# Three moves at the head of a hybrid encoder block: the second norm's spread, the third norm's sums, and a copy of the stream

## The chip, the cores and the metric

The kernel runs on one core of a Trainium2 chip. A core has five engines that run beside each other, each through its own list of instructions in order: TensorE (PE in the profile, with PEld for its weight loads), VectorE (DVE), ScalarE (ACT), GpSimd (POOL) and SyncE (SP, which here only issues transfers). They wait for each other through semaphores. The metric is the device time of one execution in microseconds. Three runs of the kernel before took 1533.51, 1535.86 and 1537.61 us, a median of 1535.86.

## The reference

The block takes 1024 frames of 1024 features, puts 16 learned meta tokens ahead of them, and runs one layer of two parts, each on a normalised stream and each added back to it.

```python
def rmsnorm(x, g):
    xf = x.astype(jnp.float32)
    y = xf * lax.rsqrt(jnp.mean(xf * xf, axis=-1, keepdims=True) + EPS)
    return (y * g.astype(jnp.float32)).astype(x.dtype)
...
    proj = up @ w_in
    (ml_q, ml_k, ml_v, ml_o, ml_i, ml_f, rt_q, rt_k, rt_v, rt_g) = jnp.split(proj, offs, axis=-1)
...
    rq = rotary(rt_q.astype(jnp.float32).reshape(b, lp, RT_HEADS, RT_DQK), pos)
    rk = rotary(rt_k.astype(jnp.float32).reshape(b, lp, RT_HEADS, RT_DQK), pos)
...
    h = jnp.concatenate([meta, x], axis=1)
    for l in range(DEPTH):
        h = h + token_mixer(rmsnorm(h, norm_mix_g[l]), ...)
        h = h + channel_mixer(rmsnorm(h, norm_ffn_g[l]), w_up[l], w_gate[l], ffn_conv_w[l], w_down[l])
    return rmsnorm(h, norm_final_g)[:, N_META:]
```

The token mixer projects the normalised stream to queries, keys, values and gates for eight heads: four of an mLSTM (with a convolution on queries and keys and exponential gates) and four of a retention (with rotary positions on queries and keys). The channel mixer is a gated MLP with a convolution. Only the first norm and the first products of the token mixer matter here.

## The kernel before

**Number form.** The products run in a fast 32-bit format that keeps fewer bits than float32. So each operand is split in a high part (a cast on ACT, names with `h` or `hi`) and a low part (original minus high part, on DVE, names with `l` or `lo`), and a product is done as high x high, high x low and low x high. Larger products are saved by a Winograd-style scheme with seven products instead of eight; it needs sums of quarters of the normalised stream, named S1 to S4.

**The head.** The stream lies in four tiles `x11`, `x12`, `x21`, `x22` (token half, then feature half), features on the partitions. It arrives and is normalised in five ranges of tokens (`RNG`: 144, 128 and 256 tokens of the first half, 272 and 256 of the second). For each range there are three steps:

- `norm_sums`: the squares are added (L855 on ACT, L859 or L863, L867 and L870 on DVE), PE adds them over the partitions (L826, tiles `pca0` to `pca4`), ACT takes the root (L828) and DVE the reciprocal (L829).
- `norm_rows`: PE hands the reciprocals to all partitions, the "spread" (L838, tiles `pra0` to `pra4`).
- `norm_split`: DVE scales the stream by it (L890, eight instructions), ACT casts the high parts (L891), DVE makes the low parts (L895).

In the rows below the tile's last digits are left out, so `pra`, `pca` and `pv` stand for all ranges. Between these steps PE does the first products on what is ready: `v4_group(c)` makes the values and gate columns of head 4 for chunk c (tile `pv4_c`, L952, 24 products of 264 columns), with the weights `w0hi` and `w0lo`; `v4_group(0)` does it for the 16 meta tokens in plain float32 with 32-column tiles (L938, eight products on `ug` and `w0raw`, named the meta products). Their four partial sums are added into `vz` by `quads`: a copy on ACT (L924) and three adds on DVE (L927). `q4_pair` makes queries and keys of head 4 for the first 272 tokens (tiles `pq4000` and `pq4100`, L977, 48 products in three passes over high and low parts); it calls `norm_sums` and `norm_rows` of the third range between its passes. `q4_group` makes them for the other tokens (L901 to L903).

**Behind the head.** `usum` forms S1 to S4 on DVE in the tiles of the stream, and `usplit` splits them (L1822 on ACT, L1823 on DVE). S1 is first formed in `s1`, two tiles that take the slots A1 and A2. S4's sums end up in `x12`, and a copy of them (L1844) goes to two other tiles, named `s4`, from which S4 is split. When S1 has been split, the slots A1 and A2 are reused for the rotary position tables `rot`, loaded by `tables_load(4)` (L1134 and L1135). The products of the output gate of head 4 (`po4x`, `po4y`, L911 to L913) then run in seven steps n = 0 to 6 over the blocks 11, 12, S2, S1, S3, S4 and 22; their results are collected in `sig`: a copy on ACT for n = 0 (L1000), a negated copy on ACT for n = 2 and 3 (L1002), an add on DVE for the others (L1004). Beside them run the rotary products of head 4 (L1209 to L1214) and `gates`, a chain of small DVE and ACT instructions on the gate columns. From there on PE goes through the query, value and output-gate weights of the other heads, the scans over the chunks, the output projection and the MLP.

**What sets the order.** Weights come in through slots (`raw...`, L328 on SP's queue); a load is issued when its slot's last reader is done, and SP issues in order, so a load that waits holds up those behind it. A helper `after(a, b)` sets instruction a behind b on its engine without a semaphore; the last instruction of a kind is kept in `last`. Where nothing is said, a list scheduler with its own cost model orders each engine's instructions when the program is built. From the output gate of head 4 on (`dealt`, `pinned`) the order is that of a planner which deals side work between PE's steps.

Of the kernel before, what the change touches and what calls it, by code (L numbers as in the profile page):

```python
# [20 lines left out]
META = 16  # L21
# [68 lines left out]
def body(ctx, tc, h_in, vecs, cst, mask_in, rot, w_v0, w_vp, w_g, w_out, w_up, w_gate, w_down, out):  # L90
# [14 lines left out]
    def after(later, first):  # L105
        dep(later, first, False)

    last = {}
# [118 lines left out]
    w0raw = (A1, A2)  # L227
# [651 lines left out]
    def norm_rows(r):  # L879
        norms[r] += (rms_rows(norms[r][1], None, "upd"),)  # L880
# [40 lines left out]

    def quads(dst, pv, n):
        yield
        AC.copy(dst, pv[:META, :n])  # L924
        yield
        for j in range(1, 4):
            V.tensor_tensor(dst, pv[32 * j:32 * j + META, :n], dst, ALU.add)  # L927
# [3 lines left out]
    def v4_group(c, tag, between=None):  # L931
        t0, L = CH[c]
        nv = 264
        pv = pp(f"pv4_{c}", tag)
        if c == 0:
            for i in range(2):
                for j in range(4):
                    PE.matmul(pv[32 * j:32 * j + 32, :nv], ug[:, 4 * i + j, :], w0raw[i][:, j * nv:(j + 1) * nv],  # L938
                                     start=i == 0, stop=i == 1, tile_position=(0, 32 * j))
            t = vz[:META, 264:264 + nv]  # L940
            spawn(quads(t, pv, nv))
            V.tensor_copy(gts[:META, :, 0, :], t[:, DV:].rearrange("p (a b) -> p a b", a=2))
            return
        half = c > 4
        j0 = t0 - 512 * half
        for i, j in ((0, 0), (0, 1), (1, 0)):
            if i and between:
                between()
            for kb in range(KB):
                u = UB[f"{half + 1}{kb // 4 + 1}"][i]  # L950
                o = kb % 4 * nv
                m = PE.matmul(pv[:, :nv], u[:, kb % 4, j0:j0 + L], (w0hi, w0lo)[j][kb // 4][:, o:o + nv], start=i + j + kb == 0, stop=i == 1 and kb == KB - 1, skip_group_check=True)  # L952
                if i and between:
                    after(m, last["rows"])
        AC.copy(vtile[4][half][:, (c - 1) % 4 * VW:(c - 1) % 4 * VW + DV], pv[:, :DV])
        V.tensor_copy(gts[:, :, c, :], pv[:, DV:nv].rearrange("p (a b) -> p a b", a=2))
# [9 lines left out]
    def q4_pair(half, j0, j1, tags, between):  # L966
        w = [need(("q4", i), 1 - i) for i in range(2)]
        pt = [pp(f"pq4{i}{half}{j0}", tags[i])[:, :j1 - j0] for i in range(2)]
        for p, (a, b) in enumerate(((0, 0), (0, 1), (1, 0))):
            if p == 2:  # L970
                between()
            for i in range(2):
                if p == 2 and i:
                    norm_rows(2)
                for kb in range(KB):
                    u = UB[f"{half + 1}{kb // 4 + 1}"][b]
                    m = PE.matmul(pt[i], w[i][kb // 4][a][:, kb % 4 * P:(kb % 4 + 1) * P], u[:, kb % 4, j0:j1], start=p + kb == 0, stop=p == 2 and kb == KB - 1, skip_group_check=True)  # L977
                    if p == 2:
                        after(m, last["rows" if i else "sums"])
        AC.copy(raws[0][:, half * 512 + j0:half * 512 + j1], pt[0])  # L980
        yield
        after(AC.copy(raws[1][:, half * 512 + j0:half * 512 + j1], pt[1]), last["cast"])
# [825 lines left out]
    def part(x, i):  # L1808
        return s1[i] if x == "S1" else xf[x][:, 2 * i:2 * i + 2]
# [31 lines left out]
    x12 = [vslot(2 + i, f"s4_{i}").rearrange("p (k j) -> p k j", k=2) for i in range(2)]  # L1841
    tables_load(4)
    for i in range(2):
        G.tensor_copy(x12[i], part("12", i))  # L1844
    s1[:] = x12
    need(("o", 4, 1))
    usplit("S4", "S1", "uh2", "ul2")
# [719 lines left out]
```

## Time and profile before

| | |
|---|---|
| median of three runs | 1535.86 us (1533.51 to 1537.61) |
| profiled execution | 1534.49 us, span 1532.7 us |
| granted PE clock, mean | 0.994 |
| PE busy | 1491.9 us, 97% of the span |
| DVE, ACT, POOL busy | 71%, 49%, 6% |
| mean DMA rate | 146 GB/s |

The profile is that of one execution. A row of the timeline has the start in us from the span's start, the busy time in us, the engine, the line, the operation, out<-in by the program's names, sizes, and the number of instructions merged in it; in brackets stands the idle time of the engine before it and what ended it. Matmuls overlap, so a row of several lasts less than the sum of its parts. A float32 product counts as two instructions in these rows.

### The profile page before, as it was taken

The numbers are of one execution on the slowest core, as the hardware profiler recorded it, in microseconds if no ns is written. First come the engines' busy times: TensorE is split into PE (matmuls) and PEld (weight loads), VectorE is DVE, ScalarE is ACT, GpSimd is POOL, SyncE is SP. The second block draws the span as 40 slices with busy tenths as digits, with TensorE's granted clock in tenths as the row PEclk, the third lists the DMA queues.
The fourth block names the chain that finished last, engine by engine and source line by source line (L and its number), as shares of the span: only waits on it lengthen the run. The fifth ranks groups of instructions, "written<-read, shape, count | busy, mean of one in ns | idle before, by whom it ended". The sixth has DMA issues, their size and how long they took to land.

```text
span 1532.7 us, 25492 instructions
## 1 busy us (share of the span) xinstructions
PE 1491.9 (97%) x9929; PEld 1351.0 (88%) x9929; DVE 1089.5 (71%) x2087; ACT 754.8 (49%) x1453; POOL 84.7 (6%) x159
## 2 busy tenths in 40 slices
PE   6979999999999999999999999999999999999997
PEld 5978999999999999997888988999999999888887
DVE  5875777767777768756868697677666666778657
ACT  4455655564655445544454465444444444434443
POOL 1020000000000000000000001222220000000000
PEclk9999999999999999999999999999999999999999
DMA  6022245323542354598333237787872224933313
GB/s 231 1 83 57 84 138 182 126 93 116 174 138 84 124 179 166 192 373 301 111 110 133 82 118 212 206 213 196 200 183 84 79 80 146 382 100 114 97 42 111
DMA packets 104586, 223.81 MB, mean 146 GB/s; under 512 B 10520, under 2 KB 33760, under 8 KB 104288
## 3 DMA queue, kind: packets, MB, share of 16 engines
q1 hardware_dynamic: 89824, 191.68, 37.3%
q0 software_dynamic: 8448, 23.07, 7.4%
q10 hardware_dynamic: 6192, 7.41, 1.4%
q8 instruction: 78, 1.28, 0.3%
q14 instruction: 44, 0.36, 0.1%
HBM read 178.05 MB, written 67.15 MB: 160 GB/s over the span
## 4 chain that ended last, share of the span: by engine, by line
PE 88%; DVE 6%; DMA 3%; ACT 2%; issue 1%; SPq 0%; DVEq 0%; ACTq 0%
PE pdx L913 3%; PE pdx L912 3%; PE pdx L911 3%; PE pup_x L912 2%; PE pup_x L913 2%; PE pup_x L911 2%; PE pga_x L911 2%; PE pga_x L912 2%; PE pga_x L913 2%; PE pdy L913 2%; PE pdy L912 2%; PE pdy L911 2%; PE n L1602 2%; PE pwx L913 2%; PE u L1600 2%; PE pwx L911 2%
## 5 line engine op out<-in xcount | busy, mean ns | idle before, releaser
L782 ACT CAST hi_up<-raw_up 128x512 fp32r<-128x512 f32 (+1 forms) x52 | 36.4, 719 | 107.3 <-PE pga_z L912 61.1
L911 PE MATMUL pup_x<-uh_g,hi_up 128*128 128x256 f32 (+1 forms) x240 | 67.6, 284 | 1.2 <-ACT uh_g L1964 1.2
L783 DVE TENSOR_TENSOR lo_up<-raw_up,hi_up 128x512 fp32r<-128x512 f32 (+1 forms) x52 | 41.2, 808 | 38.1 <-ACT hi_up L782 37.3
L783 DVE TENSOR_TENSOR lo_ga<-fraw_ga,hi_ga 128x512 fp32r<-128x512 f32 (+1 forms) x52 | 41.8, 807 | 36.7 <-ACT hi_ga L782 36.5
L912 PE MATMUL pup_x<-ul_g,hi_up 128*128 128x256 f32 (+1 forms) x240 | 67.7, 284 | 0.1
L913 PE MATMUL pup_x<-uh_g,lo_up 128*128 128x256 f32 (+1 forms) x240 | 66.7, 283 | 0.0
L783 DVE TENSOR_TENSOR lo_d<-rd,hi_d 128x1024 fp32r<-128x1024 f32 (+1 forms) x34 | 37.6, 1112 | 32.8 <-ACT hi_d L782 32.7
L782 ACT CAST hi_ga<-fraw_ga 128x512 fp32r<-128x512 f32 (+1 forms) x52 | 36.4, 719 | 45.5 <-PE pup_z L912 24.3
L913 PE MATMUL pdx<-uh_d,lo_d 128*128 128x512 f32 (+1 forms) x156 | 57.9, 375 | 0.0
L912 PE MATMUL pdx<-ul_d,hi_d 128*128 128x512 f32 (+1 forms) x156 | 57.8, 374 | 0.0
L782 ACT CAST hi_d<-rd 128x1024 fp32r<-128x1024 f32 (+1 forms) x34 | 32.3, 959 | 49.3 <-PE pdy L912 32.5
L913 PE MATMUL pdy<-uh_d,lo_d 128*128 128x512 f32 x132 | 51.9, 393 | 0.0
L912 PE MATMUL pdy<-ul_d,hi_d 128*128 128x512 f32 x132 | 51.7, 392 | 0.0
L911 PE MATMUL pdx<-uh_d,hi_d 128*128 128x512 f32 (+1 forms) x156 | 48.5, 372 | 0.0
L911 PE MATMUL pdy<-uh_d,hi_d 128*128 128x512 f32 x132 | 47.9, 389 | 0.0
L911 PEld LDWEIGHTS pup_x<-uh_g,hi_up 128*128 128x128 f32 x240 | 45.7, 191 | 2.3 <-ACT uh_g L1964 1.4
L911 PE MATMUL pga_x<-uh_g,hi_ga 128*128 128x512 f32 x120 | 47.5, 396 | 0.0
L912 PE MATMUL pga_x<-ul_g,hi_ga 128*128 128x512 f32 x120 | 47.5, 396 | 0.0
L913 PE MATMUL pga_x<-uh_g,lo_ga 128*128 128x512 f32 x120 | 47.1, 393 | 0.0
L912 PEld LDWEIGHTS pup_x<-ul_g,hi_up 128*128 128x128 f32 x240 | 45.8, 191 | 1.0 <-DVE ul_g L1965 0.3
L913 PEld LDWEIGHTS pup_x<-uh_g,lo_up 128*128 128x128 f32 x240 | 45.1, 190 | 0.8
L662 POOL DMA_DIRECT2D wsd<-w_down_d x33 | 19.9, 748 | 383.4 <-DVE s2up L2192 382.7
(1698 smaller groups left out, 5758.1 us busy)
## 6 DMA issues: line engine op xcount, KB each, us to landing
raw_up<-w_up_d SPq DMA_DIRECT2D x22, 512.0 KB, 5.2
fraw_ga<-w_gate_d SPq DMA_DIRECT2D x22, 512.0 KB, 4.2
acts<-cv SPq DMA_DIRECT2D x44, 256.0 KB, 4.3
wsd<-w_down_d POOLq DMA_DIRECT2D x44, 256.0 KB, 6.6
rd<-wsd SPq DMA_DIRECT2D x22, 512.0 KB, 3.5
raw_w<-w_out_d SPq DMA_DIRECT2D x20, 512.0 KB, 6.9
wsw<-raw_w SPq DMA_DIRECT2D x32, 256.0 KB, 3.6
raw_m<-w_out_d SPq DMA_DIRECT2D x14, 512.0 KB, 4.0
```

Of the source, the lines that this page charges most:

```text
L662: dep(G.dma_start(x, y), last["pace"], True)
L782: AC.copy(hi[:, o:o + n], x)
L783: V.tensor_tensor(lo[:, o:o + n], x, hi[:, o:o + n].bitcast(F32), ALU.subtract)
L911: m.append(PE.matmul(pt, ah, xh_, start=first and k == 0, stop=False, skip_group_check=True))
L912: PE.matmul(pt, ah, xl_, start=False, stop=False, skip_group_check=True)
L913: m.append(PE.matmul(pt, al, xh_, start=False, stop=last and k == n - 1, skip_group_check=True))
L1600: PE.matmul(up[:, :nv], kw[:L], v, start=True, stop=True)
L1602: PE.matmul(pn[:L, :nv], pt[:L, :L], v, start=True, stop=c == 0)
```

## The change

It has three parts. In `v4_group` the meta products are set behind the second norm's spread, and in `quads` the copy of their result behind the last cast of a norm. In `q4_pair` the third norm's sums come ahead of the first pass of the query and key products, not ahead of the third, and its spread behind the first pass, not in the middle of the third; the passes are set behind them. And the copy of S4's sums into their own tiles is done by ACT and no longer by POOL.

```diff
     def quads(dst, pv, n):
         yield
-        AC.copy(dst, pv[:META, :n])
+        m = AC.copy(dst, pv[:META, :n])
+        if not dealt[0]:
+            after(m, last["cast"])
         yield
...
             for i in range(2):
                 for j in range(4):
-                    PE.matmul(pv[32 * j:32 * j + 32, :nv], ug[:, 4 * i + j, :], w0raw[i][:, j * nv:(j + 1) * nv],
-                                     start=i == 0, stop=i == 1, tile_position=(0, 32 * j))
+                    after(PE.matmul(pv[32 * j:32 * j + 32, :nv], ug[:, 4 * i + j, :], w0raw[i][:, j * nv:(j + 1) * nv],
+                                    start=i == 0, stop=i == 1, tile_position=(0, 32 * j)), last["rows"])
...
         for p, (a, b) in enumerate(((0, 0), (0, 1), (1, 0))):
-            if p == 2:
+            if p == 0:
                 between()
+            if p == 1:
+                norm_rows(2)
             for i in range(2):
-                if p == 2 and i:
-                    norm_rows(2)
                 for kb in range(KB):
                     u = UB[f"{half + 1}{kb // 4 + 1}"][b]
                     m = PE.matmul(pt[i], w[i][kb // 4][a][:, kb % 4 * P:(kb % 4 + 1) * P], u[:, kb % 4, j0:j1], start=p + kb == 0, stop=p == 2 and kb == KB - 1, skip_group_check=True)
-                    if p == 2:
-                        after(m, last["rows" if i else "sums"])
+                    after(m, last["rows" if p else "sums"])
...
     for i in range(2):
-        G.tensor_copy(x12[i], part("12", i))
+        AC.copy(x12[i], part("12", i))
     s1[:] = x12
```

The number of products stays the same; ACT has two instructions more and POOL two fewer. Beyond 125 us only six products of one group at the start of the MLP change places among themselves. In the head and just behind it the scheduler comes to another order at several places. Three of them follow; a row is a line, an operation, out<-in with the program's buffer numbers, and a size, and x4 stands for four like it in a row.

PE at the end of the products of chunk 1 (`pv_1`), before: the meta products (`pv_0`) are dealt among the last low-weight products, and the spread of the second norm (`pra_285`) comes behind them.

```order
L952 MATMUL pv_1_254<-w0lo_109,u12h 128x264
L938 MATMUL pv_0_309<-w0raw_104,ug 32x264
L952 MATMUL pv_1_254<-w0lo_109,u12h 128x264
L938 MATMUL pv_0_309<-w0raw_104,ug 32x264 x2
L952 MATMUL pv_1_254<-w0lo_109,u12h 128x264
L938 MATMUL pv_0_309<-w0raw_104,ug 32x264
L938 MATMUL pv_0_309<-w0raw_105,ug 32x264
L952 MATMUL pv_1_254<-w0lo_109,u12h 128x264
L938 MATMUL pv_0_309<-w0raw_105,ug 32x264 x2
L838 MATMUL pra_285<-cs,rcola_273 128x128
```

The same place now:

```order
L954 MATMUL pv_1_254<-w0lo_109,u12h 128x264 x4
L838 MATMUL pra_285<-cs,rcola_273 128x128
L954 MATMUL pv_1_254<-w0hiq,u11l 128x264 x4
L954 MATMUL pv_1_254<-w0hik,u12l 128x264 x4
L940 MATMUL pv_0_309<-w0raw_104,ug 32x264 x4
L940 MATMUL pv_0_309<-w0raw_105,ug 32x264 x4
```

The spread has moved ahead of all meta products, and these stand together behind the products of chunk 1.

PE at the fourth norm's spread (`pra_514`), which no edit names, before: it stands near the end of the query products for tokens 272 to 528 (`pq_542`), and 26 products follow it (three of `pq_542`, 23 of the keys, `pq_568`) until the first product of the second half (`pv_5`).

```order
L901 MATMUL pq_542<-u12h,hi_q_0_0_354 128x256
L902 MATMUL pq_542<-u12l,hi_q_0_0_354 128x256
L903 MATMUL pq_542<-u12h,lo_q_0_0_355 128x256
L838 MATMUL pra_514<-cs,rcola_450 128x16
L838 MATMUL pra_514<-cs,rcola_450 128x128 x2
L901 MATMUL pq_542<-u12h,hi_q_0_0_354 128x256
L902 MATMUL pq_542<-u12l,hi_q_0_0_354 128x256
L903 MATMUL pq_542<-u12h,lo_q_0_0_355 128x256
L902 MATMUL pq_568<-u11l,hi_q_1_0_362 128x256
```

Now:

```order
L901 MATMUL pq_568<-u11h,hi_q_1_0_362 128x256
L902 MATMUL pq_568<-u11l,hi_q_1_0_362 128x256
L903 MATMUL pq_568<-u11h,lo_q_1_0_363 128x256
L838 MATMUL pra_514<-cs,rcola_450 128x16
L838 MATMUL pra_514<-cs,rcola_450 128x128 x2
L901 MATMUL pq_568<-u12h,hi_q_1_0_362 128x256
L902 MATMUL pq_568<-u12l,hi_q_1_0_362 128x256
L903 MATMUL pq_568<-u12h,lo_q_1_0_363 128x256
```

It has moved into the middle of the key products: 12 products follow it until `pv_5`.

ACT behind the sums S1 to S4 (`s_0` of L1822 is the first half of S1 or of S4 by the name on the left; `raw_o4a` and `raw_o4b` are weights of the output gate), before:

```order
L1822 CAST uS3h<-x_120 128x1056 x2
L474 CAST hi_o_4_0_873<-raw_o4b 128x512 x2
L964 COPY rawk<-pq_823 128x256
L1000 COPY sig<-po4x_887 128x258
L1822 CAST uS1h<-s_0_609 128x1056
L1822 CAST uS1h<-s_1_610 128x1056
L1000 COPY sig<-po4x_901 128x256
L1822 CAST uS4h<-s_0_855 128x1056
L1822 CAST uS4h<-s_1_856 128x1056
L474 CAST hi_o_2_0_863<-raw_o4a 128x512
```

and now, with the two copies (L1845) in between:

```order
L1823 CAST uS3h<-x_120 128x1056 x2
L1845 COPY s_0_855<-x_121 128x1056
L474 CAST hi_o_4_0_873<-raw_o4b 128x512 x2
L966 COPY rawk<-pq_823 128x256
L1001 COPY sig<-po4x_887 128x258
L1845 COPY s_1_856<-x_121 128x1056
L1823 CAST uS1h<-s_0_609 128x1056
L1823 CAST uS1h<-s_1_610 128x1056
L1823 CAST uS4h<-s_0_855 128x1056
L1823 CAST uS4h<-s_1_856 128x1056
L474 CAST hi_o_2_0_863<-raw_o4a 128x512
L1001 COPY sig<-po4x_901 128x256
```

The copies stand ahead of the casts of `hi_o_4` and of S1, and one copy out of `po4x` has gone behind a weight cast.

SP's queue at the same place, before (`A_4` are the two position tables):

```order
L328 DMA raw_vp_21_1268<-w_vp_d 128x1024
L328 DMA raw_vp_22_1270<-w_vp_d 128x1024
L1134 DMA A_4_857<-rot_d 128x1040
L1135 DMA A_4_858<-rot_d 128x1040
L328 DMA raw_q0b<-w_g_d 128x512 x2
```

and now:

```order
L1135 DMA A_4_857<-rot_d 128x1040
L1136 DMA A_4_858<-rot_d 128x1040
L328 DMA raw_vp_21_1268<-w_vp_d 128x1024
L328 DMA raw_vp_22_1270<-w_vp_d 128x1024
L328 DMA raw_q0b<-w_g_d 128x512 x2
```

The tables have moved ahead of the two value weights.

## The prediction

> **What bounds the kernel now.** I read the page first, then busy time by stage, then the chain of work that ended last, and last the timeline of the first 110 us, where the moved instructions stand. The page:
>
> ```profile
> span 1532.7 us, 25492 instructions
> ...
> PE 1491.9 (97%) x9929; PEld 1351.0 (88%) x9929; DVE 1089.5 (71%) x2087; ACT 754.8 (49%) x1453; POOL 84.7 (6%) x159
> ...
> PE 88%; DVE 6%; DMA 3%; ACT 2%; issue 1%; SPq 0%; DVEq 0%; ACTq 0%
> ```
>
> TensorE (PE) carries the kernel. The change adds and removes no product, so it can only fill PE's idle time, and that lies in few places. Busy time by stage (stretch, length, then PE, PEld, DVE, ACT, POOL, granted clock, DMA share, GB/s):
>
> ```profile
> 0.00:40.00 40.00, 28.23 (x172) 24.28 (x173) 23.74 (x53) 18.48 (x30) 7.36 (x20) 1.00 0.64 221
> ...
> 77.00:102.00 25.00, 17.93 (x133) 16.07 (x132) 17.45 (x27) 13.98 (x26) 9.43 (x2) 0.91 0.37 127
> ...
> 125.00:1532.00 1407.00, 1386.68 (x9148) 1252.46 (x9146) 999.11 (x1906) 695.23 (x1349) 64.61 (x134) 1.00 0.48 150
> ```
>
> PE idles 11.8 us before 40 and 7.1 us between 77 and 102; in the 1407 us after 125 it loses 20 us in all. So what is won or lost by 102 should reach the end. The chain of work names what holds the second stretch, and prices a product (36 in 4.51 us, 0.125 us each):
>
> ```profile
> 39.08 4.51 PE pv L952 x36
> ...
> 84.90 10.07 DMA A<-rot_d
> ```
>
> **The second norm's spread.** Seven of the eight meta products stand between the last pv4_1 products with the lower weights and the spread (pra1, which hands the scales to all partitions). DVE waits for it:
>
> ```profile
> 18.06 0.42 PE L952 MATMUL pv<-w0lo,u12h 128*128 128x264 f32 x1
> ...
> 21.99 0.49 PE L838 MATMUL pra<-cs,rcola 128*128 128x128 f32 x2
> ...
> 22.52 2.15 DVE L890 SCALAR_TENSOR_TENSOR x<-x,vec,pra 128x128 f32<-128x128 f32 x8 [4.81 <-PE pra L838]
> ...
> 24.99 0.76 PE L952 MATMUL pv<-w0hiq,u11h 128*128 128x264 f32 x4 [0.98 <-ACT u11h L891]
> ```
>
> Now four products are left ahead of pra1: 18.06 + 4 x 0.125 = 18.56, and DVE scales 0.53 later (22.52 - 21.99), at 19.1, done at 21.25. PE does eight more products (to 19.8) and then the meta products in one piece. Their price is between two rows: 3.65 us if each costs what it does now (21.99 - 18.06 less three products, for seven, times 8/7) and 1.07 us if they run like sixteen such passes that do stand together:
>
> ```profile
> 82.83 1.07 PE L722 MATMUL pvm<-raw_vm,ug 128*32 128x256 f32 x16
> ```
>
> The second has the same form, so I take it with 0.4 us for the change of shape: PE is free at 21.3. ACT's cast u11h, after the first half of the scaling (20.2) and a copy, ends by 21.0. The pv4_2 products start at 21.3, not 24.99. The copy of vz, moved behind the casts, has DVE adds as its only reader, and those have moved later too.
>
> **The third norm.** Now the sums (pca2) stand ahead of all 48 query products, and the spread (pra2) behind the first 16:
>
> ```profile
> 26.78 1.21 DVE L867 TENSOR_TENSOR sqr<-sqr,sqr 128x1024 f32<-128x1024 f32 x1
> 28.39 0.67 DVE L870 TENSOR_TENSOR sqr<-sqr 128x512 f32<-128x512 f32 x1
> 28.98 2.48 DVE L479 TENSOR_TENSOR lo_q<-raw_q,hi_q 128x512 fp32r<-128x512 f32 x4
> ...
> 32.04 0.95 PE L826 MATMUL pca<-cs,sqr 128*128 128x1 f32 x8
> ...
> 34.58 3.22 DVE L890 SCALAR_TENSOR_TENSOR x<-x,vec,pra 128x256 f32<-128x256 f32 x8 [1.09 <-PE pra L838]
> ...
> 35.19 1.12 ACT L474 CAST hi_o<-raw_o4a 128x512 fp32r<-128x512 f32 x2
> ...
> 37.60 1.24 PE L952 MATMUL pv<-w0hiq,u11h 128*128 128x264 f32 x8 [2.04 <-ACT u11h L891]
> ```
>
> DVE: scaling to 21.25, the low parts u11l and u12l (0.62 each, as the lo_q rows of 512 columns, behind the second cast) to 22.6, then 1.21, a vz add of about 0.4 and 0.67: squares at 24.9. PE is through its 24 pv4_2 products at 24.3, waits 0.6, does the sums to 25.9 and 16 products to 27.9. The reciprocal stands behind the four lo_q: 24.9 + 2.48, two small rows and itself, 28.1. So pra2 at 28.1, the scaling at 28.65 against 34.58. PE does pra2 (0.5) and 32 products (4.0): 32.6. ACT's next cast has hi_o ahead of it, which waits for a weight transfer; its slot is freed by the second lo_q, at 26.15:
>
> ```profile
> raw_o4a<-w_g_d SPq DMA_DIRECT2D x1, 512.0 KB, 3.8
> ```
>
> It lands at 29.95, the casts last to 31.1, u11h to 32.2. PE is later, so pv4_3 starts at 32.6, not 37.60: 5.0 us.
>
> Part of it is given back. The fourth norm's spread, pra3, now has 12 products behind it instead of 26, so it comes 14 products (1.75 us) later against its neighbours:
>
> ```profile
> 48.46 3.36 DVE L890 SCALAR_TENSOR_TENSOR x<-x,vec,pra 128x272 f32<-128x272 f32 x8
> ...
> 50.22 1.11 ACT L891 CAST u21h<-x 128x1088 fp32r<-128x1088 f32 x1 [1.03 <-DVE x L890]
> ...
> 51.38 1.24 PE L952 MATMUL pv<-w0hiq,u21h 128*128 128x264 f32 x8
> ```
>
> Before, cast and PE met at 51.3. Now PE is there 5.0 us early and the cast 5.0 - 1.75: PE waits 1.75. **Head: 3.2 us.** From here to 77 PE's order is the old one.
>
> **The copy and the tables.** (Times here are those of before; the head's 3.2 us comes off all of them.) POOL's two copies take 1.06 and 11.38 us:
>
> ```profile
> L1844 POOL COPY s<-x x2: 1062/6220/11377, 74.0 to 85.4; 128x1056 f32<-128x1056 f32 x2
> ...
> 74.95 2.05 ACT L1822 CAST uS3h<-x 128x1056 fp32r<-128x1056 f32 x2
> ...
> 77.94 0.37 ACT L964 COPY rawk<-pq 128x256 f32<-128x256 f32 x1
> ...
> 78.36 0.39 PE L911 MATMUL po4x<-u11h,hi_o 128*128 128x256 f32 x1 [0.98 <-ACT rawk L964]
> ...
> 82.06 2.42 DVE L1823 TENSOR_TENSOR uS1l<-s,uS1h 128x1056 fp32r<-128x1056 f32 x2
> ...
> 88.11 0.39 PE L911 MATMUL po4y<-uS1h,hi_o 128*128 128x258 f32 x1 [1.18 <-ACT hi_o L474]
> ```
>
> On ACT a copy of this shape costs 1.05 (half of 2.05). The first stands ahead of hi_o4_4 and rawk, so PE's wait at 78.36 grows by 1.05. Behind it: 77.0 + 1.05 + 1.12 + 0.37 + 0.39, the second copy, and the uS1h casts end at 82.0 and 83.0. DVE wants them at 82.06 and 83.27, so uS1l keeps its place, with 0.1 to spare. The uS4h casts follow at once, done at 85.1 (they waited for POOL to 85.45), and the waits at 88.11 and behind it go. But these PE waits were covered: PE next stands for the position tables.
>
> The tables A sit in the slots that uS1l reads last. On SP's queue they stood behind two raw_vp loads, which wait for PE's pvm; now they stand ahead of those:
>
> ```profile
> 82.18 0.33 SPq L328 DMA_DIRECT2D raw_q0a<-w_g_d  x1
> 83.53 0.81 SPq L328 DMA_DIRECT2D raw_vp<-w_vp_d  x2
> 84.43 0.38 SPq L1134 DMA_DIRECT2D A<-rot_d  x1
> ...
> 93.72 0.71 DVE L1212 TENSOR_TENSOR qT<-rawq,A 128x528 f32<-128x528 f32 x1 [3.12 <-DMA A<-rot_d]
> ...
> 95.06 0.71 DVE L1213 TENSOR_TENSOR kT<-kT,A 128x528 f32<-128x528 f32 x1 [0.64 <-DMA A<-rot_d]
> ...
> 101.28 0.58 PE L911 MATMUL po4y<-uS4h,hi_o 128*128 128x258 f32 x1 [3.35 <-ACT sig L1002]
> ```
>
> The second table can be issued at 82.06 + 2.42 = 84.5 as before, but with 0.5 MB ahead of it rather than 1.5. Its landing lies between 5.5 us, two loads of this size one behind the other, and the 10.07 of now:
>
> ```profile
> w0raw<-w_v_d SPq DMA_DIRECT2D x2, 528.0 KB, 5.5
> ```
>
> I take 5.5, the like case: 90.0. DVE is free about then: 84.5, two uS4l (2.42), two lo_o (1.24), two adds (at most 1.24) and qT give 90.1. From kT to PE's product is 6.2 us of DVE and ACT in turn (101.28 - 95.06), unchanged. PE gets there at 94.5 by its products and waits, so the start is 96.2: **5.0 us.** The raw_vp loads come later by the two tables' bytes; their readers stand behind the query products past 110. On POOL nothing is queued behind the copies that is wanted before 118.
>
> **Sum.** 3.2 + 5.0 = 8.2 us. The profiled execution took 1534.49, which gives 1526.3; it lies 1.4 under the median of the three runs, so the forecast for a median is 1535.86 - 8.2 = **1527.7**.
>
> **Rivals.** (1) The tables land no sooner: 10.07 from their issue at 84.5, because the queue and not the order sets it. For it: that row. Against: 0.5 MB ahead instead of 1.5. Then 0.5 + 3.2: 1532.2. (2) raw_o4a lands late, so that ACT's hi_o casts hold back u11h. From 7.5 us instead of 3.8 the head gives nothing, and 5.0 is left: 1530.9. Against: no load is in flight then. (3) The new wait of 1.75 us lowers PE's clock. After the waits near 88 to 90 it fell, with no wait above 1.5 us:
>
> ```profile
> 90.00:92.00 2.00, 1.95 (x12) 1.85 (x13) 0.59 (x1) 0.53 (x2) 0.00 (x0) 0.71 0.93 364
> 92.00:94.00 2.00, 2.00 (x11) 2.00 (x10) 0.28 (x1) 0.00 (x0) 0.00 (x0) 0.50 0.84 316
> 94.00:96.00 2.00, 2.00 (x17) 1.90 (x16) 1.32 (x3) 1.45 (x3) 0.00 (x0) 0.94 0.13 45
> ```
>
> That is 2 x (0.29 + 0.50 + 0.06) = 1.7 us lost; the same after the new wait leaves 6.5: 1529.4. Against: the wait of 2.04 at 37.60 left the first stage's clock at 1.00. The Trainium skill (TensorE: Matmul & The Clock Gate, section "Why this matters for your kernels") asks only that no gap exceed about 3 us. By it this rival is void and the sum stays 8.2; these three rows disagree with it, since two shorter waits close together sufficed. (4) Slower: the copy costs ACT what it cost POOL. One copy of 11.38 puts 10.3 us ahead of uS1h, hence of the tables; from 8.3 it outweighs the rest, and at 10.3 the time is 1537.9, with both copies 1548. Against: ACT's casts of that shape took 1.03 each beside the same busy DVE. (5) The change moves the work and the end stays, some later wait taking it up: 1535.9. For it only the 20 us of later idle.
>
> **Chances and range.** Forecast 0.62; rivals in order 0.11, 0.09, 0.08, 0.06, 0.04. A change under 0.3% (4.6 us, below 1531.25) is what a measurement of this kernel cannot tell from none. Faster: 0.62 + 0.08 + most of rival 2 = 0.77; same: rivals 1 and 5 and the rest of 2, 0.17; slower 0.06. Range: downward the give-back not biting (5.0 for the head) and DVE 0.6 sooner, 10.6 us, less the 2.4 by which the lowest run lies under the median: 1523. Upward it takes in rival 1: 1533.
>
> **What would show it.** Right: pra1 near 18.6; PE's pv4_3 near 32.6; a wait of about 1.7 on u21h near 48; the tables read near 87 (90.0 - 3.2); the product on uS4h near 93. Wrong: hi_o waiting for raw_o4a past 32; the tables issued near 81 and read only past 90; an ACT copy above 2 us; or all of these as said and the idle after 125 above 28 us.

## The result, and the profile after

The changed kernel took 1527.69 us (median of 5 runs, 1526.2 to 1529.07) beside 1536.96 us (5 runs, 1533.51 to 1538.01) for the kernel before: a ratio of 0.9944, 95% interval 0.9929 to 0.9958. Run again, as the base of the last experiments, it gave 0.9957 (0.9944 to 0.9970). By these two medians it is faster by 0.4 to 0.6%, 6.6 to 8.6 us; both intervals lie below 1. The profiled execution took 1526.2 us.

The page, and busy time by stage (the same columns and, but for the end, the same stretches as before):

```profile
span 1524.4 us, 25487 instructions
...
PE 1486.6 (98%) x9929; PEld 1348.3 (88%) x9929; DVE 1090.0 (72%) x2087; ACT 756.4 (50%) x1455; POOL 72.1 (5%) x157
...
PE 88%; DVE 7%; DMA 3%; ACT 1%; issue 1%; DVEq 0%; SPq 0%; ACTq 0%
```

```profile
0.00:40.00 40.00, 31.09 (x212) 29.45 (x213) 26.86 (x57) 19.23 (x32) 7.35 (x20) 1.00 0.66 222
...
77.00:102.00 25.00, 20.41 (x175) 19.09 (x174) 22.00 (x49) 18.02 (x30) 0.00 (x0) 1.00 0.38 127
125.00:1524.00 1399.00, 1379.35 (x9109) 1246.14 (x9109) 997.47 (x1900) 693.08 (x1345) 64.39 (x134) 1.00 0.48 150
```

PE idles 8.9 us before 40 (11.8 before) and 4.6 us between 77 and 102 (7.1 before). Behind 125 it loses 19.7 us, as before (20.3).

The head, in the timeline of the changed kernel:

```profile
18.88 0.63 PE L838 MATMUL pra<-cs,rcola 128*128 128x128 f32 x2
19.55 2.16 DVE L890 SCALAR_TENSOR_TENSOR x<-x,vec,pra 128x128 f32<-128x128 f32 x8 [1.91 <-PE pra L838]
20.72 1.10 PE L940 MATMUL pv<-w0raw,ug 128*32 128x264 f32 x16
21.77 0.75 PE L954 MATMUL pv<-w0hiq,u11h 128*128 128x264 f32 x4
25.33 1.05 PE L826 MATMUL pca<-cs,sqr 128*128 128x1 f32 x8 [0.21 <-DVE sqr L870]
28.47 0.71 PE L838 MATMUL pra<-cs,rcola 128*128 128x128 f32 x4
29.22 3.22 DVE L890 SCALAR_TENSOR_TENSOR x<-x,vec,pra 128x256 f32<-128x256 f32 x8
30.69 1.14 ACT L474 CAST hi_o<-raw_o4a 128x512 fp32r<-128x512 f32 x2 [2.00 <-DMA raw_o4a<-w_g_d]
33.02 1.13 PE L954 MATMUL pv<-w0hiq,u11h 128*128 128x264 f32 x8
48.23 1.24 PE L954 MATMUL pv<-w0hiq,u21h 128*128 128x264 f32 x8 [1.53 <-ACT u21h L891]
56.21 0.61 PE L838 MATMUL pra<-cs,rcola 128*128 128x128 f32 x4
56.85 3.22 DVE L890 SCALAR_TENSOR_TENSOR x<-x,vec,pra 128x256 f32<-128x256 f32 x8
```

The pv4_3 products start at 33.02 (before 37.60), 4.6 us early; at 48.23 PE waits 1.53 us for the cast u21h, and 3.15 us are left (before 51.38). The fifth norm's scaling, which stood at 60.00, stands at 56.85: 3.15 us too.

The copy and the tables:

```profile
73.75 1.07 ACT L1845 COPY s<-x 128x1056 f32<-128x1056 f32 x1
76.18 0.39 PE L911 MATMUL po4x<-u11h,hi_o 128*128 128x256 f32 x1 [1.95 <-ACT rawk L966]
81.49 0.33 SPq L1136 DMA_DIRECT2D A<-rot_d  x1
81.92 0.86 SPq L328 DMA_DIRECT2D raw_vp<-w_vp_d  x2
86.73 0.71 DVE L1214 TENSOR_TENSOR kT<-kT,A 128x528 f32<-128x528 f32 x1 [0.57 <-DMA A<-rot_d]
89.68 1.28 ACT L1245 ACT_TABLE_LOAD   x1 [1.23 <-DVE gsm L1244]
92.95 0.39 PE L911 MATMUL po4y<-uS4h,hi_o 128*128 128x258 f32 x1 [2.31 <-ACT sig L1003]
```

The second table is issued at 81.49 and read at 86.73; the product on uS4h comes at 92.95 instead of 101.28. Of these 8.33 us, 5.18 lie behind the head. On the chain of waits the second table now stands with 5.15 us instead of 10.07:

```profile
81.49 5.15 DMA A<-rot_d
```

### The profile page after: what moved, and what is told of

Read it like the earlier page. It is cut to its first block, busy times and chain, and to the rows that moved or that the text cites. A ratio compares the mean times of both kernels' runs of the same rounds, so it can differ in the third digit from the quotient of the medians.

```text
span 1524.4 us, 25487 instructions
## 1 busy us (share of the span) xinstructions
PE 1486.6 (98%) x9929; PEld 1348.3 (88%) x9929; DVE 1090.0 (72%) x2087; ACT 756.4 (50%) x1455; POOL 72.1 (5%) x157
## 4 chain that ended last, share of the span: by engine, by line
PE 88%; DVE 7%; DMA 3%; ACT 1%; issue 1%; DVEq 0%; SPq 0%; ACTq 0%
PE pdx L913 3%; PE pdx L912 3%; PE pdx L911 3%; PE pup_x L912 2%; PE pga_x L911 2%; PE pup_x L913 2%; PE pup_x L911 2%; PE pga_x L912 2%; PE pga_x L913 2%; PE pdy L913 2%; PE pdy L912 2%; PE pdy L911 2%; PE n L1603 2%; PE pwx L913 2%; PE u L1601 2%; PE pwx L911 2%
## 5 line engine op out<-in xcount | busy, mean ns | idle before, releaser
L1670 DVE SCALAR_TENSOR_TENSOR mx<-tr,vec,sig 128x386 f32<-128x386 f32 (+2 forms) x42 | 24.0, 571 | 21.5 <-PE tr L1662 16.0
```

What stands on the lines that cost most here:

```text
L1670: return V.scalar_tensor_tensor(dst, tr[:, x0 - t0:x1 - t0], vec[:, g:g + 1], sig(b, p)[:, x0 - a0:x1 - a0], ALU.mult, ALU.mult)
```

## The experiments

The theory: the head's new order gives 3.2 us, and the tables' place ahead of the two value weights on SP's queue gives 5.0. Its rivals: POOL's slow copy was the cost of the second part; the head does it all. One table holds what the runs showed. Its first three columns are starts in the profiled execution less those of the kernel before: the issue of raw_q0a (82.18 before; the head's end), the product on uS4h (101.28), the issue of raw_o0a (168.30; everything the change touches is over by then). The fourth lists where PE's granted clock was 0.50 before 125 us (the start; each lasts 3.41 us, those marked x2 twice that; this halved clock is called half clock below); the last is the ratio to the kernel before over all runs, with its interval.

| kernel | raw_q0a | uS4h | raw_o0a | half clock at | ratio |
|---|---|---|---|---|---|
| before | 0 | 0 | 0 | 90.8, 101.1 | 1 |
| changed | -3.15 | -8.33 | -7.75 | 102.0 | 0.9944 (0.9929 to 0.9958) |
| changed, again | -1.60 | -6.67 | -6.83 | 50.2, 94.6 | 0.9957 (0.9944 to 0.9970) |
| head | -2.88 | -4.09 | -2.84 | 95.9 x2 | 0.9978 (0.9967 to 0.9990) |
| copy | -0.24 | -4.98 | -3.59 | 80.4, 104.3 x2 | 0.9984 (0.9972 to 0.9996) |
| tables_back | -1.60 | -3.33 | -3.47 | 50.0, 94.4 x2 | 0.9985 (0.9975 to 0.9995) |
| tables_front | +2.74 | -1.19 | -1.22 | 93.8 | 0.9976 (0.9965 to 0.9987) |
| meta | -4.06 | -5.18 | -3.77 | 93.9 x2 | 0.9975 (0.9966 to 0.9984) |
| third | +0.51 | -0.14 | +1.51 | 30.9, 99.1 x2 | 1.0008 (0.9999 to 1.0018) |
| spread4 | -2.71 | -7.77 | -7.30 | 102.3 | 0.9954 (0.9942 to 0.9966) |
| clock_fill | -1.63 | -6.90 | -7.40 | 50.4, 77.7 | 0.9959 (0.9947 to 0.9971) |
| copy_late | -2.96 | -6.83 | -6.74 | 102.9 | 0.9956 (0.9943 to 0.9969) |
| gates_first | -3.22 | -10.03 | -8.97 | 112.2 | 0.9951 (0.9936 to 0.9965) |
| bias_fill | -2.78 | -8.88 | -7.68 | 76.7, 124.5 | 0.9950 (0.9937 to 0.9963) |

**head: the two norms' edits alone.** The change without this:

```diff
-        G.tensor_copy(x12[i], part("12", i))
+        AC.copy(x12[i], part("12", i))
```

> The kernel before with the edits to the second and third norm alone; the copy of S4's sums stays on POOL, and SP's queue keeps its old order (both value weights ahead of both tables). Theory: the head is worth 3.2 us (ratio 0.998), pv4_3 starts near 33 and PE waits some 1.5 us on u21h near 48; the tables are still read about 10 us after their issue, and the product on uS4h comes at 98.1 (101.28 less 3.2). Rival 'the head does it all': 8.3 us less than before (ratio 0.9946), with the tables early here too.

Measured 3.4 us (0.9978). PE waits 1.53 us on u21h, and the tables are read 8.95 us after their issue (82.02 to 90.97):

```profile
97.19 0.58 PE L911 MATMUL po4y<-uS4h,hi_o 128*128 128x258 f32 x1 [3.38 <-ACT sig L1003]
```

The head alone is not the whole. But 1.21 of the 4.09 us at this product lie behind raw_q0a, where nothing had been forecast (97.19 for 98.1): the second table lands 8.86 us after its issue here, not 10.07, though both value weights stand ahead of it as before. Why it lands sooner was not tried.

**copy: ACT does the copy, the head is the old one.** Of the change, those two lines alone.

> The kernel before with the copy on ACT alone; the head is the old one. On SP's queue both tables now stand ahead of the two value weights. Theory: 5.0 us less than before (ratio 0.9967); the second table lands about 5.5 us after its issue and is read near 90; the product on uS4h at 96.2. Rival 'the head does it all': no change (ratio 1.000).

```profile
90.08 0.71 DVE L1213 TENSOR_TENSOR kT<-kT,A 128x528 f32<-128x528 f32 x1 [1.01 <-DMA A<-rot_d]
...
96.30 0.39 PE L911 MATMUL po4y<-uS4h,hi_o 128*128 128x258 f32 x1 [1.21 <-ACT sig L1002]
```

Up to this product the trace is as expected: 4.98 us for 5.0, 90.08 for 90, 96.30 for 96.2. From 104.3 on the clock is at 0.50 for 6.83 us, on the next heads' query products, and 3.6 us are left at 168. The ratio says 2.5 us (0.6 to 4.3), half of what was expected.

**tables_back: the changed kernel with the old order on SP.**

```diff
-            nc.sync.dma_start(x[:, o:o + y.shape[1]], y)
+            m = nc.sync.dma_start(x[:, o:o + y.shape[1]], y)
+            if nm in ("vp0_21", "vp0_22"):
+                for t in loads4:
+                    after(t, m)
...
-            nc.sync.dma_start(A1, rot[:, 0])
-            nc.sync.dma_start(A2, rot[:, 1])
+            for x, y in ((A1, rot[:, 0]), (A2, rot[:, 1])):
+                m = nc.sync.dma_start(x, y)
+                if h == 4:
+                    loads4.append(m)
```

> The changed kernel with one thing put back: on SP's queue the two value weights stand ahead of the two tables again. All other engines keep the order of the changed kernel, and ACT still does the copy. Theory (the queue's order is what the second part is worth): the second table lands about 10 us after its issue, is read at 91.5 to 92 (before: 95.06, less the head's 3.2) and the product on uS4h comes near 98; time 3.2 us less than before (ratio 0.998), so 5 us more than the changed kernel. Rival 'POOL's slow copy was the cost': the order of the queue makes no difference, 8.3 us less than before (0.9946).

```profile
91.73 0.71 DVE L1220 TENSOR_TENSOR kT<-kT,A 128x528 f32<-128x528 f32 x1 [0.65 <-DMA A<-rot_d]
...
97.95 0.58 PE L915 MATMUL po4y<-uS4h,hi_o 128*128 128x258 f32 x1 [3.35 <-ACT sig L1007]
```

The two rows come where they were expected, 91.73 and 97.95 for 91.5 to 92 and 98, and the ratio is 0.9985. That the places agree is in part luck. This execution has a half-clock stretch at 50.0, and its head ends 1.55 us later than in the changed kernel's first trace (raw_q0a at 80.58 for 79.03); and the second table lands 7.37 us after its issue (84.27), not some 10. The trace to compare it with is the changed kernel's second one, which has such a stretch at 50.2 and issues raw_q0a at 80.58 too:

```profile
88.39 0.71 DVE L1214 TENSOR_TENSOR kT<-kT,A 128x528 f32<-128x528 f32 x1 [0.67 <-DMA A<-rot_d]
...
94.61 0.58 PE L911 MATMUL po4y<-uS4h,hi_o 128*128 128x258 f32 x1 [2.41 <-ACT sig L1003]
```

Between these two the order alone is worth 3.34 us, at the table, at the product and still at raw_o0a, not 5.0. Of that, 1.23 us are the table's later issue (84.27 for 83.04) and 2.1 its longer way (7.37 us for 5.25). ACT does the copy here as in the changed kernel, so the rival falls that POOL's slow copy was the cost and the order made no difference.

**tables_front: the kernel before with the tables in front on SP.** The tables are kept in `loads4` as above, and:

```diff
+            if nm in ("vp0_21", "vp0_22"):
+                after(m, loads4[-1])
```

> The kernel before with one thing changed: on SP's queue the two tables stand ahead of the two value weights. POOL still does the copy, the head is the old one. Theory: the tables land in time for a read at 90, but POOL's copy ends at 85.4 and the casts of uS4h behind it at 87.8, so uS4l, which stands on DVE ahead of the rotary products, ends at 88.9 at the earliest and the low weights and qT after it; kT is read near 91.3 and the product on uS4h comes near 97.5: 3.8 us less than before (ratio 0.9975), so the copy itself is worth some 1.2 us. Rival 'POOL's slow copy was the cost': no change (1.000).

This execution was 2.74 us late at raw_q0a, for a reason in the first 26 us (last section); that comes off its times.

```profile
76.78 12.39 POOL L1849 COPY s<-x 128x1056 f32<-128x1056 f32 x2 [42.49 <-DVE gts L959]
...
93.87 0.70 DVE L1218 TENSOR_TENSOR kT<-kT,A 128x528 f32<-128x528 f32 x1
...
100.09 0.38 PE L914 MATMUL po4y<-uS4h,hi_o 128*128 128x258 f32 x1
```

kT is read at 91.1 on the kernel before's clock, that is less 2.74 (expected 91.3), without a wait for the table, and the product comes at 97.35 (expected 97.5). At 168 it is 3.96 us ahead, and the ratio says 3.7. POOL's copy is as slow as ever, so most of the second part is to be had by the queue's order alone; ACT's copy adds about the last 1 us (copy's product stood at 96.30), because POOL's holds the casts of uS4h until 88.19 (85.45 on the kernel before's clock; in copy they start at 82.12). So the order is worth 3.3 us (tables_back) to 3.9 us (here) of the second part; the rest comes with ACT's copy and with the new head, and the shares were not taken apart further.

**meta and third: each norm's edit alone.** Of the change, in meta the lines of `quads` and `v4_group`, in third those of `q4_pair`; their cores:

```diff
-                    PE.matmul(pv[32 * j:32 * j + 32, :nv], ug[:, 4 * i + j, :], w0raw[i][:, j * nv:(j + 1) * nv],
-                                     start=i == 0, stop=i == 1, tile_position=(0, 32 * j))
+                    after(PE.matmul(pv[32 * j:32 * j + 32, :nv], ug[:, 4 * i + j, :], w0raw[i][:, j * nv:(j + 1) * nv],
+                                    start=i == 0, stop=i == 1, tile_position=(0, 32 * j)), last["rows"])
```

```diff
-            if p == 2:
+            if p == 0:
                 between()
+            if p == 1:
+                norm_rows(2)
```

> The kernel before with the second norm's edit alone (meta products behind its spread, copy of vz behind the casts). The third norm's sums keep their place ahead of the third pass; the copy of S4's sums stays on POOL. The fourth norm's spread has 12 products behind it, as in the changed kernel, and one of the two value weights stands ahead of the first table, both ahead of the second. Theory: pv4_2 starts near 21.5 as in the changed kernel, but the third sums now wait behind 32 query products, so DVE scales the third range at 31.6 (before 34.58, changed 29.22) and pv4_3 starts at 34.3 (before 37.60, changed 33.02). The cast u21h comes with the fourth spread, so the head is worth 3.15 - 1.3 = 1.9 us here; raw_q0a is issued at 80.3. With 0.5 us or so from the tables: ratio 0.9985. Rival 'the second norm's edit is the whole head': 3.2 us at raw_q0a's issue and 0.998.

> The kernel before with the third norm's edit alone. The meta products stay where they were, so the second spread stays at 21.99 and pv4_2 at 25. The fourth norm's spread has 12 products behind it, as in the changed kernel. Theory: the squares of the third range come at 29.1, the sums to 30.1, pra2 near 32.1, the scaling near 32.7 (before 34.58); PE does its query products without a wait and gets to pv4_3 at 36.6, 1.0 us early. The fourth spread gives back up to 1.75, so the product on u21h comes up to 0.75 us later than before: head between -0.3 and +0.75 us, raw_q0a's issue at 82.2 to 82.9, ratio 1.000 (0.999 to 1.001). Rival 'each norm's edit gives its own share': the rest of 3.2 us that the second norm's edit leaves, 1.3 us, ratio 0.999.

The second expectation held by the time: third alone gains nothing (1.0008). Its rows test it less well, for this execution has a half-clock stretch at 30.9, in the middle of what the edit moves (the third spread at 34.10 for 32.1, pv4_3 at 38.62 for 36.6). The first expectation fell: meta alone gives 4.06 us at raw_q0a (1.9 expected) and a ratio of 0.9975. At raw_q0a that is more than both edits together give (2.88 in head, 3.15 in the changed kernel). The product on u21h, the fifth norm's spread and its scaling, in meta and then in third:

```profile
49.17 1.24 PE L954 MATMUL pv<-w0hiq,u21h 128*128 128x264 f32 x8 [1.66 <-ACT u21h L891]
55.27 0.60 PE L838 MATMUL pra<-cs,rcola 128*128 128x128 f32 x4
55.95 3.22 DVE L890 SCALAR_TENSOR_TENSOR x<-x,vec,pra 128x256 f32<-128x256 f32 x8
```

```profile
53.83 1.24 PE L952 MATMUL pv<-w0hiq,u21h 128*128 128x264 f32 x8 [1.53 <-ACT u21h L891]
59.80 0.61 PE L838 MATMUL pra<-cs,rcola 128*128 128x128 f32 x4
60.44 3.22 DVE L890 SCALAR_TENSOR_TENSOR x<-x,vec,pra 128x256 f32<-128x256 f32 x8 [0.63 <-PE pra L838]
```

The third norm's edit does bring u21h forward, by 0.94 us (48.23 in the changed kernel). But between u21h's product and the fifth spread lie 7.98 us in the changed kernel and 6.10 in meta, since the scheduler puts 66 products between them there (as in the kernel before) and 50 in meta. What counts at raw_q0a is the fifth scaling: 56.85 changed, 55.95 meta, 60.44 third, 60.00 before, which are shifts of -3.15, -4.05 and +0.44, the first column of the table. So beside the second norm's edit the third norm's costs 0.9 us at this place in these two traces. It is not the earlier sums that cost it, but the order that the scheduler comes to with both edits: third alone has 49 products between u21h and the spread. Some of the 0.9 us is the execution: meta's PE is 0.25 us ahead of the changed kernel's before any edit bears on it (11.53 for 11.78 at the second sums), and the four other traces with the changed head and no stretch near 50 issue raw_q0a 2.78 to 3.22 us ahead. The times do not tell meta from head (0.9975 and 0.9978, intervals of 0.001 each way), so that dropping the third norm's edit would make the kernel faster is not shown. The second norm's edit with ACT's copy, without the third's, was not tried.

**spread4: the fourth spread ahead of the key products.** The key products of tokens 272 to 528 are set behind the spread (`after` with `last["rows"]`), and on DVE:

```diff
-                after(m, last["pace"] if r in (2, 3) else last["recip"])
+                after(m, last["pace"] if r in (2, 3) else last["scale"] if r == 4 else last["recip"])
```

> The changed kernel with the fourth norm's spread set ahead of the key products of tokens 272 to 528, some 11 products earlier on PE, and the fifth range's add of squares on DVE behind the fourth range's scaling. Theory (the spread's late place is what was given back): the scaling of the fourth range starts 1.3 us earlier than in the changed kernel (45.32), the wait of 1.53 us on u21h at 48.23 goes or falls under 0.3, raw_q0a is issued 1.3 us earlier (77.7), and the time is 1.3 us less than the changed kernel's: 9.6 less than before, ratio 0.9937. Rival: DVE, not PE, holds the scaling (its low parts stand ahead of it), the wait stays and the ratio is the changed kernel's 0.9945.

```profile
46.85 1.24 PE L957 MATMUL pv<-w0hiq,u21h 128*128 128x264 f32 x8
56.73 0.61 PE L838 MATMUL pra<-cs,rcola 128*128 128x128 f32 x4
57.37 3.22 DVE L890 SCALAR_TENSOR_TENSOR x<-x,vec,pra 128x256 f32<-128x256 f32 x8 [1.77 <-PE pra L838]
...
76.74 0.39 PE L914 MATMUL po4x<-u11h,hi_o 128*128 128x256 f32 x1 [3.35 <-ACT rawk L969]
```

The wait on u21h is gone, as the theory had it, and the product comes 1.38 us earlier than in the changed kernel. It gains nothing (0.9954): 78 products now lie between it and the fifth spread, 9.88 us, the fifth scaling waits 1.77 us for that spread and is 0.5 us late, and PE waits 3.35 us for rawk (1.95 in the changed kernel). Neither the theory nor the rival named this. It is the same finding as in meta: up to 76 us the fifth norm sets the pace, and with it the place that the scheduler gives its spread on PE.

**gates_first: the gate chain ahead of the rotary products.** Here the rotary products come so late that rawq and rawk already take products of the next heads: the last 248 columns of rawk take them from 113.36 on, and the rotary product `kT<-rawk` on the second half of rawk follows at 118.09. Head 4's retention is thus computed from partly other values. The run shows where PE waits; it is no faster version of the block.

```diff
-    side += qk_tasks(4)[:2] + gate_tasks + qk_tasks(4)[2:] + scan[:12]
+    side += gate_tasks + qk_tasks(4) + scan[:12]
```

> The changed kernel with the gate chain of head 4 put ahead of its rotary products on DVE and ACT. In the changed kernel PE waits 2.31 us on sig at 92.95 (ACT stands in the gate chain behind rotary) and 1.52 + 0.76 us for gates near 100. Theory: the chain starts some 5 us earlier, its wait for DVE behind the tables is gone, and both waits of PE fall under 1 us together: 3 us less than the changed kernel, ratio 0.9925. Rival: the rotary products, now behind the gate chain, come late for the scores of head 4, and PE waits for qT or kT instead: no less than the changed kernel, 0.9945 or more.

The waits of 2.31 us on sig and of 1.52 and 0.76 us ahead of the query products are gone, and the query products start at 97.58 (101.54 in the changed kernel). But DVE does the rotary products later, and with them the low weights, and PE waits there. The ratio is 0.9951 (0.9936 to 0.9965): the rival's outcome, with lo_q where the rival had qT or kT.

```profile
111.40 0.39 PE L913 MATMUL pq0y<-uS1h,lo_q 128*128 128x264 f32 x1 [2.12 <-DVE lo_q L479]
```

**after_again and clock_fill: the half-clock stretches.**

> The changed kernel once more, beside the three that follow, as their base: 0.9945 of before (1526 to 1529 us). In its first trace PE's granted clock is 0.50 from 102.0 to 105.4 and 1.00 before; all half-clock stretches of all traces so far are 3.41 us long or twice that, and lie whole multiples of 3.41 us apart within one execution. Theory: the clock is set in steps of 3.41 us by how busy PE was in the step before. Then this trace has again one such stretch or none between 75 and 125, at a place that moves by up to 3.4 us from one execution to the next.

Two stretches before 125, at 50.2 and 94.6, none at 102. Between 75 and 125 there is one, as expected, but it lies 7.4 us from the first trace's, not within 3.4. Steps of 3.41 us laid through them (stretch, length, PE, PEld, DVE, ACT, POOL, clock, DMA share, GB/s):

```profile
46.82:50.23 3.41, 1.98 (x17) 1.99 (x18) 3.41 (x8) 2.48 (x3) 0.00 (x0) 1.00 0.00 0
50.23:53.64 3.41, 3.41 (x17) 3.41 (x17) 3.41 (x6) 0.26 (x1) 0.00 (x0) 0.50 0.00 0
91.20:94.61 3.41, 1.00 (x9) 0.80 (x8) 1.57 (x7) 2.27 (x5) 0.00 (x0) 1.00 0.14 51
94.61:98.02 3.41, 3.41 (x16) 3.41 (x17) 3.30 (x9) 2.67 (x5) 0.00 (x0) 0.50 0.00 0
98.02:101.43 3.41, 3.41 (x30) 3.41 (x30) 3.19 (x11) 1.88 (x4) 0.00 (x0) 1.00 0.00 0
```

The step ahead of each has PE busy for 1.98 and 1.00 of 3.41 us. In the first trace of the same kernel the step ahead of its stretch:

```profile
98.59:102.00 3.41, 1.13 (x9) 0.77 (x8) 3.12 (x13) 1.89 (x3) 0.00 (x0) 1.00 0.00 0
102.00:105.41 3.41, 3.41 (x18) 3.41 (x17) 3.28 (x14) 0.07 (x1) 0.00 (x0) 0.50 0.00 0
```

Same kernel, and the same wait of 1.53 us on u21h in both traces (at 48.23 and 48.25); only where the steps' edges fall differs. The stretch at 50.2 costs the head 1.55 us (-1.60 instead of -3.15).

```diff
+        for kb in range(12):
+            x = UB["11"][0]
+            PE.matmul(pe[:, 128:384], x[:, kb % 4, 0:P], x[:, kb % 4, 0:256], start=True, stop=True)
         PE.transpose(pe[0:1, 0:R36], b[:, P - 1:P], ident[:R36, :R36])
```

> The changed kernel with 12 idle products (128x256, 0.12 us each, into an unused part of the tile pe, never read) ahead of the two products of pe, where PE waits 1.52 us for gates and 0.76 us for gsm in the changed kernel. They need nothing that is late, so they run inside the first wait; nothing else is moved up to the MLP. Theory (a step of 3.41 us with PE busy for less than half of it halves the clock in the next): no half-clock stretch at 100 to 108, the query products of the next heads run at 0.12 us instead of 0.42 from the start, and the time is up to 1.7 us less than the changed kernel's, some 1.3 us in the mean over executions: ratio 0.9936. Rival (the clock falls by the wait for gates itself or by something that is not PE's idle time): the stretch stays, same time as the changed kernel, and at worst 0.1 us more for the products.

No stretch between 100 and 108. But its base, the changed kernel's second trace, had none there either, and the times agree (0.9959 and 0.9957, where 0.9936 was expected): neither the theory nor that the filling saves time is shown by this run.

**copy_late: the first copy behind rawk.**

```diff
-        AC.copy(x12[i], part("12", i))
+        after(AC.copy(x12[i], part("12", i)), last["raw"])
```

> The changed kernel with ACT's first copy of S4's sums behind hi_o_4 and rawk instead of ahead of them; SP's queue keeps the changed kernel's order. Theory: PE's wait of 1.95 us on rawk at 76.18 falls to 0.98 as before, but the tables, the rotary products and the gate chain behind them come no sooner, so PE's wait of 2.31 us on sig at 92.95 grows to 3.3 us and the time is the changed kernel's (difference within 0.3 us). Rival: the wait on rawk was a cost, and the kernel is 1.0 us faster than the changed one, ratio 0.9938.

```profile
75.42 0.39 PE L914 MATMUL po4x<-u11h,hi_o 128*128 128x256 f32 x1 [0.99 <-ACT rawk L969]
...
94.45 0.39 PE L914 MATMUL po4y<-uS4h,hi_o 128*128 128x258 f32 x1 [3.30 <-ACT sig L1006]
```

As the theory had it: 0.99 and 3.30, and the same time (0.9956). The 1.05 us that the copy puts ahead of rawk are covered.

**bias_fill: clock_fill, and the gate bias computed in the head.**

```diff
-        bi = small(R36, 1)
-        V.tensor_scalar(bi, vec[:R36, V_BI:V_BI + 1], 1.0 / 15.0, None, ALU.mult)
+        bi = vec[:R36, V_N + 1:V_N + 2]
...
+    V.tensor_scalar(vec[:R36, V_N + 1:V_N + 2], vec[:R36, V_BI:V_BI + 1], 1.0 / 15.0, None, ALU.mult)
     gate_gen = gates()
```

> The kernel with the 12 idle products and one more edit: the scaled gate bias, a DVE row of 0.13 us that in the changed kernel stands behind the rotary products and three adds of vz (89.47) and holds ACT's table load by 1.23 us, is computed in the head into a spare column of vec. Theory: DVE and ACT, not PE, set the pace from the tables to the first query products of the next heads, so the gate chain comes 1.2 us earlier, PE's wait on sig at 92.95 falls from 2.31 to 1.1 us, the query products start 1.2 us earlier, and with the half-clock stretch gone the time is 1.2 + 1.3 us less than the changed kernel's: ratio 0.9928. Rival: ACT's table load then waits for PE's or DVE's next row instead, and only the idle products' part is left, 0.9936.

The query products start at 100.70, though raw_q0a is 0.37 us later than in the changed kernel's first trace: 1.2 us earlier than its head would give, as expected, and the product on uS4h (92.40) has no wait left. Then PE waits for the scans of head 4:

```profile
124.05 0.49 PE L1563 MATMUL s<-qT,kT 128*128 128x128 f32 x2 [2.15 <-DVE pt L1587]
```

That wait was 1.43 us in the changed kernel's first trace, and it is followed by a half-clock stretch at 124.5. Ratio 0.9950 (0.9937 to 0.9963), not told apart from the changed kernel's 0.9957. No kernel here is shown to beat the changed one.

## Why the prediction was right

The forecast was 1527.7; the medians are 1527.69 and 1527.88. By its steps:

- **The second norm's spread.** pra1 came at 18.88 for 18.56 and the scaling at 19.55 for 19.1. The four products ahead of pra1 took 0.22 us each, not 0.125: up to 20.07 PE's products come 0.22 us apart in this execution, and 0.12 from there on. The 0.3 us carry through. The meta products in one piece took 1.10 us for 1.07, so the far row with the same form was the right one of the two ends. (The other end, 3.65 us, works out at 4.06 if the three products in between cost 0.125 each; it was not used.)
- **The third norm.** pra2 at 28.47 for 28.1, raw_o4a landed by 30.69 for 29.95, pv4_3 at 33.02 for 32.6. PE, not ACT, was late there, as said.
- **The give-back.** 1.53 us for 1.75, and the head 3.15 for 3.2. But the prediction costed the two norms' edits as one, and that hid which of them pays: meta has the second norm's edit alone, and its trace is 0.9 us ahead of the changed kernel's at raw_q0a; third has the other alone, and gains nothing. Its sentence that PE's order behind u21h is the old one is true of the changed kernel (66 products and 7.98 us to the fifth spread in both); meta gets around it with 50.
- **The copy.** PE waits 1.95 us for rawk, where 0.98 + 1.05 was forecast; copy_late shows that it was covered, as assumed.
- **The tables.** Issue 81.49 for 81.3 (84.5 less 3.2), landing 5.15 us for 5.5, kT at 86.73 for 86.8, the product at 92.95 for 93. The part is 5.18 us for 5.0. tables_back and tables_front show that the queue's order is its main cause, with 3.3 to 3.9 us. The forecast put the whole 10.07 us of the old landing down to the 1.5 MB ahead of the table; with the same two value weights ahead it took 8.86 us in head and 7.37 in tables_back, so that the full 5.0 came out took ACT's copy and the new head as well. Rival 1 fell (5.15 us), rival 2 too (raw_o4a came 4.1 us after its issue at 26.56, not 7.5), and rival 4 (ACT's copies took 1.07 and 1.09 us).
- **The sum.** 8.2 forecast; 8.3 in the profiles. That agreement is in part luck: at 900 us the changed kernel was 6.8 us ahead, and gained 1.5 more because the kernel before's execution had a half-clock stretch at 927 and its own had none. Its second trace ends 6.1 us ahead. By the ratios the change is worth 6.6 to 8.6.
- **Rival 3**, a lower clock behind the new wait on u21h, did not show in the first trace and did in the second, at 1.55 us where 1.7 was priced. Which of the two comes is a matter of the execution: the same kernel did both. So is the stretch on the query products (102.0 in the first trace).

What the prediction missed is that these gains meet DVE and ACT again. PE still waits 2.31 us for sig, 1.52 for gates and 0.76 for gsm before the next heads' query products, and each experiment that took a wait of PE away (spread4, gates_first, copy_late, bias_fill) met another wait, of PE or of DVE, some 10 to 30 us later.

## What to carry to other kernels

Where a load lands late, look at what stands ahead of it on its queue before looking at the engine that seems slow: an edit on one engine can reorder another's queue, and here that side effect was worth 3.3 to 3.9 us, more than the copy's own share of about 1 us. Cost each part of a change against the next chain behind it (here the fifth norm on DVE), not against the wait in front of it, and test the parts singly: one of the three here gains nothing alone and comes with a later spread beside the others. When a wait of PE is shortened, look first at what PE would wait for next.

## What the runs showed of the hardware

PE's clock is granted in steps. In all 14 traces the stretches at 0.50 last 3.41 us or twice that, but for the last one of each trace, which runs past the kernel's end; and within one execution their starts lie whole multiples of 3.41 us apart over 1500 us (to under 0.01 steps); the edges fall differently in each execution. Laying that grid over every trace from 15 us to its end, the step behind one at full clock was at half clock in 33 of 33 cases where PE had been busy less than 1.5 of the 3.41 us, in 25 of 60 between 1.5 and 2.1, and in 2 of 6030 above 2.1. In between, busy time alone does not decide: near 920 us eight traces have a step with 2.08 or 2.09 us busy, and all eight are followed by half clock; near 880 us eight have one with 1.72 to 2.07, and none is. What does decide there is open. So one wait of 1.5 us can cost up to 1.7 us more, and the same wait costs nothing in another execution. The Trainium skill (TensorE: Matmul & The Clock Gate, section "What's actually happening") states a free-running window of 3413 ns; the traces agree. The Trainium skill's rule in "Why this matters for your kernels" of the same page, that no gap should exceed about 3 us, is too wide by these rows: a wait of 1.53 us, in a step with PE busy for 1.98 us, was enough (second trace, at 48.25).

The head shows the same edges. PE's first products of 264 columns come 0.22 us apart and 0.12 us apart from some edge of that execution's grid on: near 19.2 in the kernel before's trace, 20.1 in the changed kernel's, 25.5 in tables_front's, which is thereby 2.74 us late at raw_q0a. The clock column reads 1.00 ahead of that edge only because the trace's record of the clock begins there (19.15, 20.07 and 25.49); it holds no value for the first 19 to 25 us. Such differences add to those of the half-clock stretches, and so the parts' ratios need not add up to that of the whole: head and tables_front together give 0.46%, the changed kernel 0.56 and 0.43%.
